# A matrix product with a written-out order: the last visit in two parts, two early stores whole, and a new order

## The chip, the cores and the metric

The kernel runs on one core of one Trainium2 chip. The metric is the device time of one execution in microseconds (us). An execution that was profiled has, beside this time, a span: the time from its first to its last instruction in the trace. All times below that are positions ("at 7.70") count from the start of the span.

## The reference

The inputs are `input` (16 × 512 × 1024) and `grad_output` (16 × 512 × 768), both float32. What is computed is

```python
grad_weight = np.einsum('bmk,bmn->kn', input, grad_output)
```

so with all 16 × 512 = 8192 rows in one list, the result is the product of the transposed input (1024 × 8192) with the gradient (8192 × 768): 1024 × 768 numbers, float32. The sum runs over the rows.

## The kernel before, in words

**Tiles.** The 8192 rows are cut in 64 slabs of 128, which is the depth of one matmul on TensorE. Two slabs are a pair; there are 32 pairs, u = 0 to 31 (line 12: pairs 0 to 3 are of the kind "s", the others of the kind "P"). The result is cut in 1024/128 = 8 row blocks and 2 halves of 384 columns. So one matmul takes 128 × 128 numbers of the input as the stationary operand (loaded into the array by a weight load, PEld) and 128 × 384 of the gradient as the moving one, and adds its product to 128 × 384 float32 numbers in one of the eight PSUM banks, bank 0 to bank 7.

**Fewer products.** The eight slabs of pairs 0 to 3 are multiplied in the plain way. The result's four quarters are named A, B, C and D (A and B are the upper 512 rows, A and C the left 384 columns), each with q = 0 to 3 for the row block inside. That is 16 matmuls for each slab. A pair of the kind "P" is treated as a 2 × 2 block product in Winograd's form: seven products in place of eight, named 1, A, B, C, 5, 6 and 7, each with q = 0 to 3, so 28 matmuls for each pair. Products 1 and A use the loaded tiles as they are. The others need sums of the tiles, which VectorE (DVE) makes: `sum_x` in three stages from x (lines 184, 186, 188) and `sum_g` in three from g (194, 196, 198). Products 5 and 7 need stage 0 of both, 6 needs stage 1, B needs stage 2 of x and C stage 2 of g. In all there are 8 × 16 + 28 × 28 = 912 matmuls of 384 columns.

**Loads.** Slab 0 and the x part of slab 1 come as float32 through the queues of SP and ACT, and DVE and ScalarE (ACT) round them to bf16 (line 202, tokens r0 to r4). Everything else is loaded by GpSimd's (POOL's) queue and becomes bf16 on the way (lines 153 to 160): for each pair first g, then x, in the order of u. Eleven pairs are held at a time, and eight sets of sums.

**Visits.** Eight kinds (A, B, C, D, 1, 5, 6, 7) with four q each make 32 sums, and there are eight banks. So a sum comes and goes: a *visit* opens a block in a bank, a number of matmuls are added to it, and the visit is closed, which copies the bank to SBUF (tile `acc` for A to D, `macc` for 1, 5, 6 and 7, `aside` for a part put by). When it comes again, either the stored sum is first copied back to the bank by ACT ("filled", line 309), or the visit starts at zero and DVE adds bank and stored sum when it is closed (line 378). A closing is done by ACT (a copy, line 356) or by DVE (line 376 a copy, 378 an addition). A0, A1 and A2 stay in banks 5, 6 and 7 for nearly the whole kernel.

**The end.** When a sum is complete, it is added to another (product 1 to A and 6, 6 to 7, 7 to C, 5 and others to B and D: DVE in lines 360 to 371, or POOL in line 388), and the part of the result is stored through SP's queue (line 291). The first `HALVED` stores are cut in two halves of 192 columns. The very last visits are B2 and B0; DVE's line 371 closes both.

**The order.** What each of PE, DVE, ACT and POOL does, and in which order, is written out by hand in the string `PLAN`: a list of tokens that is walked once, each engine taking its own instructions in this order. Each engine works strictly in order and waits at its next instruction until what it needs is there. The tokens:

- `C0@2.1`: visit of block C0 opens in bank 2 (from zero), with 1 matmul. `A0.3`: 3 more matmuls in A0's open visit. `@R` is the lasting bank of A0, A1, A2.
- `fB2@5`: ACT fills bank 5 with the stored B2. `fB2@0+3`: ACT fills columns 0 to 255 in bank 0 and columns 256 to 383 in bank 3.
- `cB2`, `vB2`, `kC2`: the visit is closed by ACT (c), by DVE (v), or by DVE with D's sum folded in (k).
- `x0.7`, `g2.7`: stage 0 of x, stage 2 of g for pair 7, on DVE.
- `pA3`, `qA3`: POOL adds the other sum, before the last visit is closed or after it.
- `r0` to `r4`: a rounding of slab 0 or 1.

`fill` knows visits in two parts: if two banks are named, the first takes 256 columns and the second 128. `multiply` then runs, for each part, all n matmuls of the token (so the weights are loaded once for each part), and `close` handles part by part; a final visit of B, C or D in two parts stores each part by itself, the left through SP's queue and the right through ACT's. The plan before has no such visit.

Ahead of everything, TensorE runs 17 matmuls on constants (`WARMUP`, line 136) while the first loads come.

Of the kernel before, what the change touches and what calls it, by code (L numbers as in the profile page):

```python
# [9 lines left out]
P = 128  # L10
# [4 lines left out]
    "C0@2.1 A0@R.1 r0 r1 r3 B1@1.1 r2 A2@R.1 r4 A1@R.1 vB1 A1.1 D3@4.2 A0.1 C0.1 D0@3.1 B2@0.1 cC0 B2.1 D0.1 "  # L15
    "fB1@1 A2.1 B3@2.2 cD3 B1.2 B3.1 D2@4.1 cB1 D2.1 vB3 D2.1 D0.1 A0.1 C1@2.3 C2@1.4 A1.2 cC2 B2.1 C1.1 B2.1 "
    "D2.1 cC1 D1@1.2 vD2 D1.1 fD3@2 D1.1 A2.2 cD0 vD1 B0@4.1 D3.2 A3@3.2 cD3 A3.2 B0.2 vA3 B0.1 C3@1.4 B2.2 "
    "B1@3.1 B0.1 cB2 B0.1 A1.2 cB0 D2@0.2 A0.3 D0@2.3 C3.2 A2.1 C0@4.1 vC3 C0.3 B1.2 B3@1.5 B1.1 D0.1 C0.1 vB1 "
    "C0.1 A0.2 vB3 D0.1 fD3@3 D2.2 vC0 fC3@1 A2.3 vD0 fD1@4 D3.3 vD2 D3.1 D1.1 g0.4 D1.1 fC1@0 D1.2 C3.1 fA3@2 "
    "g1.4 C3.1 C1.1 vD1 cD3 C1.3 kC3 fC2@3 A3.2 g2.4 A3.1 fB2@1 A3.1 x0.4 A3.1 C2.2 cA3 C2.1 x1.4 C2.2 A2.1 "  # L20
    "x2.4 10@2.1 cC2 A0.1 C1.1 v10 12@4.1 60@3.1 cC1 B2.1 g0.5 B2.1 c12 B2.1 61@0.1 g1.5 c60 62@2.1 B0@4.1 vB2 "
    "B0.1 c61 B0.1 11@3.1 c62 A1.1 vB0 A1.1 f12@1 A1.1 13@0.1 x0.5 13.1 12.1 11.1 c13 73@4.1 x1.5 73.1 c11 "
    "50@2.2 c12 k73 51@0.1 53@3.1 c50 53.1 x2.5 A1.1 52@4.1 g0.6 c53 52.1 51.1 fB1@2 A0.1 v52 63@1.2 c51 "
    "71@3.1 g1.6 71.1 fC0@4 g2.5 B1.2 g2.6 B1.1 c63 70@0.1 k71 70.1 C0.1 f10@1 C0.1 x0.6 C0.1 c70 B3@3.2 A1.1 "
    "cC0 10.1 x1.6 10.1 cB1 72@0.1 vB3 72.1 c10 72.1 C1@4.1 x2.6 f62@3 C1.1 60@2.1 k72 60.1 cC1 61@1.2 g0.7 "
    "A0.1 fB2@4 62.1 v61 62.1 B0@0.2 c62 g1.7 B2.2 vB0 c60 C3@1.2 cB2 C3.1 g2.7 C2@3.2 x0.7 fA3@2 C2.1 12@0.1 "
    "f51@4 12.1 vC3 A3.2 cC2 A3.1 v12 51.2 cA3 70@1.1 x1.7 70.1 c51 53@0.1 g0.8 53.1 A2.1 c70 A2.1 x2.7 A2.1 "
    "fB3@2 A1.1 v53 63@4.1 fB1@1 63.1 B3.1 g1.8 B3.1 f11@3 13@0.1 v63 13.1 cB3 B1.2 g2.8 11.1 v13 C3@4.1 cB1 "
    "C3.1 A2.1 x0.8 fC1@2s 11.2 C0@1.1 f71@0 C0.1 vC3 C1.2 cC0 71.1 x1.8 71.1 c11 71.1 vC1 52@1.2 c71 52.1 "
    "g0.9 A1.1 f73@3 60@4.2 v52 50@2.1 f62@0 50.1 g1.9 50.1 f13@1 73.1 v60 73.2 c50 62.1 x2.8 62.1 72@4.1 g2.9 "  # L30
    "72.1 c62 10@2.1 x0.9 10.1 c73 10.1 13.2 f70@0s v10 A0.2 f51@3 A0.1 v72 70.2 c13 51.1 x1.9 51.1 fC2@4s "
    "61@2.1 v70 61.1 fB2@1 61.1 C2.1 x2.9 C2.1 c51 B0@0.1 g0.10 B0.1 c61 B0.1 B2.1 vC2 B2.1 f11@3 B2.1 A2.1 "
    "vB0 f71@4 A3@2.2 x0.10 A3.1 cB2 11.1 A0.1 f12@0 11.1 g1.10 A2.1 71.1 f63@1 vA3 71.1 12.1 c11 12.1 g2.10 "
    "12.1 x1.10 c71 A1.2 g0.11 63.1 c12 63.2 fB1@4 x2.10 C1@3.2 g1.11 c63 62@2.2 vC1 B1.2 fB3@1 B1.1 v62 "
    "C0@0.1 fC3@3 C0.1 B3.1 g2.11 B3.1 cB1 B3.1 x0.11 C3.2 f72@4 C3.1 vC0 13@2.2 cC3 A2.1 x1.11 72.1 cB3 72.1 "
    "v13 72.1 f50@3s 73@0.2 g0.12 73.1 f53@1 52@2.2 v73 52.1 c72 50.2 g1.12 50.1 f60@0s 53.1 v52 53.1 fC0@4s "
    "53.2 g2.12 60.1 f51@2 v50 60.2 c53 A1.1 x0.12 A0.2 fB2@3 A1.1 C0.1 v60 f10@1 51.3 x1.12 C0.1 f70@0 10.2 "
    "vC0 c51 10.1 70.2 g0.13 70.1 f61@4s C2@2.2 x2.12 c70 C2.1 61.1 x2.11 c10 61.2 vC2 B2.2 f11@1 B2.1 g1.13 "
    "B0@0.1 f12@2 v61 B0.2 11.2 vB0 f62@4 11.1 12.2 cB2 x0.13 12.1 A3@0.1 c11 A3.2 g2.13 C1@3.1 f71@1 x1.13 "
    "C1.2 vA3 62.1 c12 62.2 g0.14 71.1 f63@0 71.2 x2.13 fC3@2 A2.1 63.1 vC1 63.1 c71 63.1 C3.1 g1.14 C3.1 c63 "  # L40
    "A2.1 g2.14 B3@1.1 c62 B3.2 x0.14 C3.1 A0.2 cC3 vB3 53@4.3 fB1@2 x1.14 73@0.2 v53 73.1 f72@1 50@3.2 x2.14 "
    "50.1 B1.1 v73 72.3 v50 60@4.2 c72 60.1 g0.15 B1.1 f52@0 B1.2 v60 13@3.3 A1.1 f70@4 x0.15 A1.2 cB1 52.2 "
    "v13 52.2 70.1 g1.15 70.1 c52 x1.15 70.1 A2.1 fC2@3 A2.1 g2.15 C0@0.1 g0.16 C0.1 c70 C0.1 C2.1 fB2@2 x2.15 "
    "C2.2 vC0 B0@4.2 cC2 B2.1 g1.16 B2.2 fC1@3 g2.16 51@1.2 vB0 51.1 cB2 12@0.2 x0.16 12.1 f10@4 C1.3 v51 10.2 "
    "cC1 10.1 x1.16 10.1 61@2.1 v12 61.1 c10 61.2 x2.16 f11@1 A1.1 71@0.1 g0.17 71.1 fB3@4 71.1 v61 62@3.3 v71 "
    "B3.3 v62 53@2.2 cB3 B1@0.1 g1.17 B1.1 11.1 v53 11.3 vB1 f60@2 A3@4.3 x0.17 c11 A3.1 A2.1 f72@3 A2.1 vA3 "
    "50@0.1 70@1.2 g0.18 72.1 f13@4 72.1 50.1 x1.17 50.1 72.1 v70 13.2 c72 13.1 g1.18 60.2 g2.17 c13 60.1 v50 "
    "63@1.1 fB2@3 63.2 g2.18 63.1 f73@0 A0.1 x0.18 A0.1 f52@4 A0.2 73.1 c60 x1.18 73.2 x2.17 73.1 52.1 x2.18 "
    "63.1 c73 C0@2.2 v63 C0.1 B0@0.2 vC0 B0.2 52.1 g0.19 52.1 fA3@2 A1.2 vB0 c52 B2.3 g1.19 f61@4 10@1.1 x0.19 "
    "10.2 A3.2 g2.19 51@0.2 x1.19 cA3 51.2 v10 cB2 A2.1 61.2 f62@2 v51 61.1 C1@3.2 x2.19 fC2@0 C1.1 62.1 g0.20 "  # L50
    "62.2 B1@1.1 vC1 B1.1 c62 C2.1 g1.20 B1.1 f53@3 A2.1 A1.1 g2.20 12@2.1 c61 vB1 12.3 f11@4 x0.20 C2.2 f70@1 "
    "C2.1 53.1 v12 53.1 cC2 53.2 x1.20 11.2 v53 A2.1 70.1 c11 70.1 x2.20 70.1 fB0@3 52@2.1 g0.21 52.1 B2@0.1 "
    "c70 B2.1 B3@4.1 g1.21 B3.1 v52 B3.2 B0.1 vB2 B0.1 C3@1.2 g2.21 C3.1 fC2@0 C3.1 vB3 C3.1 cB0 C3.2 A0.1 "
    "f72@2 A0.1 vC3 A0.1 13@4.1 C2.1 x0.21 13.1 f50@1 13.2 71@3.1 g0.22 71.2 x1.21 71.2 g1.22 72.3 g2.22 72.1 "
    "v71 50.2 c72 50.2 C2.1 x0.22 fC1@2 C2.1 13.1 A1.1 f60@3 A1.1 x1.22 A1.1 cC2 C1.2 v13 c50 C1.1 60.1 x2.21 "
    "60.1 cC1 60.1 x2.22 60.1 f63@0 60.1 C0@1.2 v60 C0.2 63.1 g0.23 63.3 vC0 A0.1 B0@3.1 c63 B0.1 g1.23 61@4.1 "
    "f51@1 61.2 x0.23 62@0.1 f11@2 62.1 51.1 vB0 51.3 x1.23 11.2 v61 11.2 61@3.1 A0.1 A2.1 v61 A2.2 62.1 v11 "
    "62.1 73@4.2 g0.24 f70@2 73.3 x2.23 c51 10@3.2 v62 10.1 fA3@1 10.2 x0.24 A1.2 70.2 x1.24 70.2 v10 50@0.3 "
    "x2.24 A3.2 v50 A3.3 v73 B1@3.1 fB3@0 B1.2 g2.23 cA3 B1.1 g0.25 B1.1 c70 B3.2 vB1 B3.1 f13@1 B3.1 12@2.1 "
    "g1.25 f53@4 12.2 x0.25 12.1 f52@3 12.1 53.2 vB3 53.2 x1.25 53.1 13.2 v12 13.1 52.1 g1.24 52.1 c13 52.1 "  # L60
    "g2.25 52.1 c53 52.1 x2.25 63@2.1 A0.1 f11@0 g0.26 63.2 B2@1.1 g1.26 11.2 v63 A2.2 B2.2 f60@2 x0.26 B2.2 "
    "c11 A0.1 B0@4.1 c52 B0.1 x1.26 B0.1 60.1 g2.24 fC2@0 60.1 g2.26 60.2 71@3.2 g0.27 c60 71.1 C2.2 x2.26 "
    "C2.2 vB0 C3@2.1 B2.1 A1.1 g1.27 fC0@4 A1.1 kC2 C3.3 g2.27 C3.1 f72@0 C0.2 x0.27 C0.3 vC3 71.3 kC0 72.1 "
    "fC1@2 72.2 vB2 72.1 fA3@4 72.2 x1.27 C1.2 c72 v71 C1.3 g0.28 f73@0 62@1.3 fB3@3 kC1 62.1 A0.1 73.1 g1.28 "
    "73.1 f51@2 v62 73.2 A3.1 g2.28 A3.2 x0.28 A3.1 52@1.2 cA3 51.1 x2.27 51.1 c73 51.1 x1.28 51.2 52.1 A1.1 "
    "50@0.1 v52 50.3 v51 61@4.1 f70@1 61.2 g0.29 61.2 70.1 g1.29 70.2 v61 70.1 A2.1 A1.1 v50 B3.1 f63@4 12@2.2 "
    "x0.29 12.1 63.3 x1.29 A2.2 g2.29 A2.1 70.1 x2.28 63.1 A0.1 v12 A0.2 B3.1 k70 B3.2 B1@0.1 x2.29 B1.1 cB3 "
    "B1.1 g0.30 B1.1 c63 B1.1 10@2.2 x0.30 f60@4 10.4 vB1 60.2 53@3.1 g1.30 53.2 x1.30 53.2 g2.30 13@0.2 v53 "
    "13.2 60.2 g0.31 f72@3 A1.2 f11@1 v10 A0.1 A2.1 72.1 g1.31 72.1 f12@2 72.1 11.1 g2.31 11.1 x2.30 11.2 "
    "x0.31 11.2 A1.1 13.1 c11 13.1 x1.31 12.1 cA1 12.1 v13 12.1 A0.1 f62@1 A2.1 x2.31 10@6.1 p63 c12 72.1 60.1 "  # L70
    "v10 cA2 62.3 cA0 62.1 v60 63@7.1 f73@6 63.1 qA0 v62 A3@0.1 f70@4 A3.1 73.1 v63 73.1 f50@5 73.2 qA2 v72 "
    "70.1 f53@2 A3.1 50.1 v73 70.1 fC3@3 53.1 50.1 v70 f61@1 qA1 50.1 C3.2 v53 fC2@7 C3.2 fB3@6 C3.1 pA3 61.2 "
    "cC3 61.1 v50 C2.1 f71@4 C2.3 qC3 f51@3 C2.1 v61 71.2 cC2 71.1 vA3 71.1 fC0@1 B3.1 qC2 B3.1 v71 B3.1 fB1@7 "
    "51.2 vB3 f52@0 51.1 C0.1 pC1 C0.1 fB0@4 v51 C0.2 fB2@5 C1@2.4 vC0 B1.2 52.1 vC1 52.2 vB1 B2.3 v52 B2.2 "
    "B0.4 vB2 B0.2 vB0 "
).split()

WARMUP = [("b", 512), ("f", 512), ("f", 512)] + 14 * [("b", 128)]
PAIRS_HELD = 11
SUMS_HELD = 8  # L80
MERGED = 2
HALVED = 4
ASIDES = 7
# [5 lines left out]
def kernel(  # L89
# [8 lines left out]
    f32 = mybir.dt.float32  # L98
# [4 lines left out]
    NH = N // 2  # L103
# [237 lines left out]
    def close(engine, p, q, queue):  # L341
# [39 lines left out]
        if last(p, q) and not opened[p, q] and not (engine == "c" and p in "ABC"):  # L381
            closed.add((p, q))
# [66 lines left out]
```

## Time and profile before

| | before |
|---|---|
| median of 3 runs | 161.49 us (161.28 to 161.57) |
| the profiled execution, its own time | 161.48 us |
| its span | 159.7 us |
| mean granted TensorE clock | 0.999 |
| matmuls of the product (L331) | 576 + 336 = 912, of 128 × 384 |
| busy: PE, DVE, ACT, POOL | 154.6, 136.1, 104.4, 42.6 us |
| loads by POOL's queue (q0) | 28.64 MB, 90.7% of 16 DMA engines' span |
| stores | 12 of 192 KB, 8 of 96 KB, all through SP |

How to read it. The lines of the profile name the line of the kernel (L331 is `nc.tensor.matmul` in `multiply`), the engine, the operation, what it writes and reads, how often, the busy time and the mean of one in ns. "Idle before" is how long the engine stood still just ahead of them, and whom it waited for. The view of waits sums that up by pairs of waiter and releaser: in total, how often, the longest. The chain of waits goes back from the last instruction to what released it, step by step. The timeline lists instructions in order of time, several of a kind in one line. A DMA has an issue, which is an instruction of a queue, and a landing, when its last byte is counted.

Two other things are used below. The *order* is what stands in the built program for each engine, one instruction after another; it has no times in it. From it every matmul has a number, 1 to 912. The *landings* are the times in the trace when each load was counted complete.

### The profile page before, as it was taken

How to read it: one execution, taken by the hardware profiler on the slowest of the kernel's cores; microseconds unless marked ns; L12 is line 12 of the kernel's file. 1: busy time of each engine (PE TensorE's matmuls, PEld its weight loads, DVE VectorE, ACT ScalarE, POOL GpSimd, SP SyncE). 2: the span in 40 equal slices, each digit the busy share in tenths (PEclk: the TensorE clock that was granted, in tenths of full speed). 3: DMA queues.
4: the chain of work that ended last, by engine and by line, in shares of the span. 5: the costliest groups of instructions: out<-in, count | busy, mean ns of one | idle time of the engine just before them, and what ended most of it. 6: DMA issues, size and time to landing. Idle time of an engine off the chain costs nothing.

```text
span 159.7 us, 2734 instructions
## 1 busy us (share of the span) xinstructions
PE 154.6 (97%) x931; PEld 91.2 (57%) x931; DVE 136.1 (85%) x316; ACT 104.4 (65%) x243; POOL 42.6 (27%) x77
## 2 busy tenths in 40 slices
PE   8899999999999999999999999999999999999990
PEld 3456656556555565665656565656566565656560
DVE  0514169999999999999999999989999899999992
ACT  3445238999999999967867585563465472339930
POOL 7442222222212222221222221222222100006930
PEclk9999999999999999999999999999999999999999
DMA  5999999999999999999999999999999999940696
GB/s 171 297 212 211 214 216 212 213 213 212 213 213 211 214 212 213 214 211 214 213 214 212 214 213 214 212 211 213 213 211 219 208 214 213 213 81 0 196 353 239
DMA packets 12829, 33.40 MB, mean 209 GB/s; under 512 B 1424, under 2 KB 4624, under 8 KB 12816
## 3 DMA queue, kind: packets, MB, share of 16 engines
q0 software_dynamic: 9360, 28.64, 90.7%
q1 hardware_dynamic: 3168, 3.54, 6.6%
q10 hardware_dynamic: 288, 1.05, 1.7%
q8 instruction: 7, 0.11, 0.3%
q14 instruction: 6, 0.05, 0.1%
HBM read 58.72 MB, written 3.15 MB: 387 GB/s over the span
## 4 chain that ended last, share of the span: by engine, by line
PE 91%; DMA 4%; DVE 2%; issue 1%; ACT 0%; ACTq 0%; DVEq 0%
PE bank L331 91%; DMA xf<-in_input_dram 4%; DVE acc L371 1%; DVE macc L364 0%; DVE xp L202 0%; ACT macc L356 0%; ACTq L129 0%; DVE acc L378 0%; DVE acc L366 0%; DVEq L371 0%
## 5 line engine op out<-in xcount | busy, mean ns | idle before, releaser
L331 PE MATMUL bank<-gp,xp 128*128 128x384 bf16 x576 | 105.4, 326 | 0.7 <-DVE xp L202 0.6
L331 PEld LDWEIGHTS <-xp 128*128 128x128 bf16 x576 | 55.8, 98 | 39.1 <-DVE xp L202 1.0
L331 PE MATMUL bank<-ge,xe 128*128 128x384 bf16 x336 | 65.9, 326 | 0.0
L331 PEld LDWEIGHTS <-xe 128*128 128x128 bf16 x336 | 32.7, 98 | 22.3 <-DVE xe L184 0.6
L309 ACT COPY bank<-macc 128x384 f32<-128x384 f32 x69 | 32.6, 489 | 10.4 <-DVE macc L378 6.2
L356 ACT COPY macc<-bank 128x384 f32<-128x384 f32 x64 | 29.4, 484 | 10.4 <-PE bank L331 10.1
L378 DVE TENSOR_TENSOR macc<-bank,macc 128x384 f32<-128x384 f32 x56 | 30.5, 554 | 1.2 <-PE bank L331 0.9
L154 POOL DMA_DIRECT2D xp<-in_input_dram x30 | 15.9, 529 | 52.6 <-DMA xp<-in_input_dram 21.9
L309 ACT COPY bank<-acc 128x384 f32<-128x384 f32 x46 | 21.8, 485 | 11.5 <-DVE acc L378 8.9
L356 ACT COPY acc<-bank 128x384 f32<-128x384 f32 x44 | 20.7, 480 | 11.4 <-PE bank L331 11.1
L153 POOL DMA_DIRECT2D gp<-in_grad_output_dram x30 | 15.9, 531 | 38.4 <-PE bank L331 17.2
L378 DVE TENSOR_TENSOR acc<-bank,acc 128x384 f32<-128x384 f32 x42 | 22.8, 553 | 1.9 <-PE bank L331 1.9
L184 DVE TENSOR_TENSOR xe<-xp 128x1024 bf16<-128x1024 bf16 x28 | 19.3, 689 | 1.0 <-DMA xp<-in_input_dram 0.9
L194 DVE TENSOR_TENSOR ge<-gp 128x768 bf16<-128x768 bf16 x28 | 15.5, 552 | 0.2 <-DMA gp<-in_grad_output_dram 0.2
L376 DVE COPY acc<-bank 128x384 f32<-128x384 f32 x9 | 5.0, 555 | 8.9 <-PE bank L331 8.9
L186 DVE TENSOR_TENSOR xe<-xe,xp 128x512 bf16<-128x512 bf16 x28 | 11.8, 421 | 0.3
L188 DVE TENSOR_TENSOR xp<-xp,xe 128x512 bf16<-128x512 bf16 x28 | 11.5, 419 | 0.0
L196 DVE TENSOR_TENSOR ge<-gp,ge 128x384 bf16<-128x384 bf16 x28 | 9.9, 353 | 0.2
L198 DVE TENSOR_TENSOR gp<-ge,gp 128x384 bf16<-128x384 bf16 x28 | 9.8, 354 | 0.2
L388 POOL TENSOR_TENSOR acc<-acc,macc 128x384 f32<-128x384 f32 x7 | 6.8, 1003 | 0.5 <-ACT acc L356 0.5
L388 POOL TENSOR_TENSOR macc<-macc 128x384 f32<-128x384 f32 x1 | 1.0, 1042 | 18.0 <-DVE macc L378 18.0
L202 DVE CAST gp<-gf 128x192 bf16<-128x192 f32 (+1 forms) x2 | 0.6, 310 | 4.9 <-DMA gf<-in_grad_output_dram 4.9
(23 smaller groups left out, 41.2 us busy)
## 6 DMA issues: line engine op xcount, KB each, us to landing
xp<-in_input_dram POOLq DMA_DIRECT2D x30, 512.0 KB, 16.7
gp<-in_grad_output_dram POOLq DMA_DIRECT2D x30, 384.0 KB, 16.7
out_dram<-acc SPq DMA_DIRECT2D x12, 192.0 KB, 2.1
xf<-in_input_dram ACTq DMA_DIRECT2D x2, 512.0 KB, 4.9
out_dram<-acc SPq DMA_DIRECT2D x8, 96.0 KB, 1.7
gp<-in_grad_output_dram POOLq DMA_DIRECT2D x3, 192.0 KB, 6.4
xp<-in_input_dram POOLq DMA_DIRECT2D x2, 256.0 KB, 7.8
gf<-in_grad_output_dram SPq DMA_DIRECT2D x2, 192.0 KB, 4.1
```

What stands on the lines that cost most here:

```text
L153: nc.gpsimd.dma_start(out=gp, in_=G[rows, :].rearrange("(p m) n -> p m n", m=2))
L154: nc.gpsimd.dma_start(out=xp, in_=X[rows, :].rearrange("(p m) k -> p m k", m=2))
L184: nc.vector.tensor_sub(out=xe[:, 0:2, :], in0=x[:, 1::-1, :], in1=x[:, 3::-2, :])
L186: nc.vector.tensor_sub(out=xe[:, 2, :], in0=xe[:, 0, :], in1=x[:, 0, :])
L188: nc.vector.tensor_add(out=x[:, 1, :], in0=x[:, 2, :], in1=xe[:, 2, :])
L194: nc.vector.tensor_add(out=ge[:, 0:2, :], in0=g[:, 0:2, :], in1=g[:, 1::2, :])
L196: nc.vector.tensor_add(out=ge[:, 2, :], in0=g[:, 3, :], in1=ge[:, 0, :])
L198: nc.vector.tensor_add(out=g[:, 1, :], in0=ge[:, 2, :], in1=g[:, 2, :])
L309: nc.scalar.copy(out=tile_[:, at : at + c1 - c0], in_=src[:, c0:c1])
L331: nc.tensor.matmul(tile_[:, at : at + c1 - c0], stat, mov[:, c0:c1], start=fresh, stop=True, skip_group_check=True,)
L356: nc.scalar.copy(out=to, in_=b)
L378: nc.vector.tensor_add(out=to, in0=b, in1=to)
```

## The change

The diff changes the string `PLAN` throughout, two numbers, the banks of the warm-up, and how a closing by ACT of a block that POOL has already added to is treated. (The new plan has no such closing: its `p` tokens are pA3 and p70, and both visits are closed by DVE.)

```diff
 PLAN = (
-    "C0@2.1 A0@R.1 r0 r1 r3 B1@1.1 r2 A2@R.1 r4 A1@R.1 vB1 A1.1 D3@4.2 A0.1 C0.1 D0@3.1 B2@0.1 cC0 B2.1 D0.1 "
...
-    "51.2 vB3 f52@0 51.1 C0.1 pC1 C0.1 fB0@4 v51 C0.2 fB2@5 C1@2.4 vC0 B1.2 52.1 vC1 52.2 vB1 B2.3 v52 B2.2 "
-    "B0.4 vB2 B0.2 vB0 "
+    "C0@0.1 A1@R.1 A0@R.1 r0 C1@3.1 B1@4.1 B3@1.1 r1 r4 cC1 B3.1 A2@R.1 r3 A2.1 vB3 C0@2.1 vC0 r2 D3@0.2 "
+    "C3@1.3 C0.1 A1.1 cC3 A1.1 vC0 C2@3.2 D3.1 A0.2 cD3 C2.1 C1@2.2 vC2 D1@0.4 fB3@3 A3@1.4 C1.1 B3.1 vA3 B3.1 "
...
+    "71.1 v61 71.1 fC1@6 71.2 v52 cB3 71.1 C2.1 f51@7 C2.1 qB3 C2.2 fB1@2 v71 C2.1 51.1 fB2@0+3 51.1 vC2 B1.3 "
+    "fB0@1 v51 C1.4 B0.2 vC1 B0.3 vB1 B2.3 vB0 B2.5 vB2 "
 ).split()
...
-HALVED = 4
+HALVED = 3
...
-    wps = psum.tile([P, 512], f32, name="bank7")
-    for dt, cols in WARMUP:
+    wps = [psum.tile([P, 512], f32, name=f"bank{b}") for b in (7, 4)]
+    for n, (dt, cols) in enumerate(WARMUP):
...
-            wps[:, 0:cols],
+            wps[n % 2][:, 0:cols],
...
+                assert (p, q) not in prepared or (final and carried and len(parts) == 1)
                 nc.scalar.copy(out=to, in_=b)
...
-        if last(p, q) and not opened[p, q] and not (engine == "c" and p in "ABC"):
+        if final and engine == "c" and (p, q) in prepared:
+            store(p, q, 0, NH, queue)
+        if last(p, q) and not opened[p, q] and (engine != "c" or p not in "ABC" or (p, q) in prepared):
             closed.add((p, q))
```

With `HALVED` 3 in place of 4, one store of 192 KB that was two issues of 96 KB is one. The last visit is now B2's, with eight matmuls for each of its two parts (`fB2@0+3`, `B2.3`, `B2.5`), 256 columns and 128 columns wide. So TensorE has 904 matmuls of 384 columns, 8 of 256 and 8 of 128. Ahead of it stand C1's last visit (4 matmuls), B0's (5, the first two before vC1) and, in DVE's order, v51, vC1, vB1 and vB0. SP has 6 stores of 192 columns, 12 of 384 and one of 256; ACT's queue has one of 128, the right part of B2. The order of POOL's loads is as it was; the last additions on POOL are eight as before (two p, six q, for three and five).

At the start, the first eleven matmuls are C0, A1, A0, C1, B1, B3 on slab 0, then B3 on slab 1, A2 on slab 0, A2 and C0 on slab 1, and D3 on slab 0 in bank 0. On DVE the first closings are vB3 (bank 1) and then vC0 (bank 0).

## The prediction

> **What bounds the kernel now.** I began with the page: its engine line and chain of waits say that TensorE is nearly all of the span.
>
> ```profile
> PE 154.6 (97%) x931; PEld 91.2 (57%) x931; DVE 136.1 (85%) x316; ACT 104.4 (65%) x243; POOL 42.6 (27%) x77
> PE 91%; DMA 4%; DVE 2%; issue 1%; ACT 0%; ACTq 0%; DVEq 0%
> q8 instruction: 7, 0.11, 0.3%
> ```
>
> A busy PE does not say that more work could have been done sooner, so I listed the starts of the 912 real matmuls (L331). The first starts at 5.91 us, the 912th at 155.75. A step between two that nothing delays is 0.1625 us (mean of 895 of the 911 steps), so 911 of them are 148.0 and 1.8 us are stalls: 1.0 before 7.70, the rest in a few steps, of which the view of waits names these:
>
> ```profile
> PEld L331 <- DVE xp L202: 1.0, 1, 1.0
> PEld L331 <- DMA xp<-in_input_dram: 1.0, 4, 0.3
> PEld L331 <- DVE xe L184: 0.6, 2, 0.4
> ```
>
> TensorE waits for loads and for the sums made from them, in the middle of the kernel. The loads come at a rhythm of their own: the x part of pair u lands at 16.16 (u=2), 20.50, 25.60, 29.91 and then every 4.31 us (47.44 for u=9, 64.70 for 13, 138.03 for 30, 142.53 for 31). One pair is 28 matmuls, 4.55 us of TensorE: little more than the rhythm of its load.
>
> So I made one table from the orders and the landings. If the first matmul that needs load u is number n, the 912th can't start before E = landing + 0.05 + (912 − n) × 0.1625; the 0.05 is the usual delay from landing to first use (51.75 to 51.79, 34.22 to 34.27). If it needs a sum made by L184, add 0.69 for that and 0.05 for its wait. For the kernel before, the largest E is 155.75, from pair 27: x lands at 125.70, 0.62 later than the rhythm asks, and matmul 732 needs its sum. 125.70 + 0.05 + 0.69 + 0.05 leaves 126.49, and 180 × 0.1625 = 29.25 more is 155.74. The 912th started at 155.754: this one landing set the end. The next largest E that the same late landing does not touch is 155.31 (u=10). The timeline shows the place, first DVE and then the weight loads:
>
> ```profile
> 125.73 0.69 DVE L184 TENSOR_TENSOR xe<-xp 128x1024 bf16<-128x1024 bf16 x1 [0.70 <-DMA xp<-in_input_dram]
> ```
> ```profile
> 126.47 0.93 PEld L331 LDWEIGHTS <-xe 128*128 128x128 bf16 x7 [0.38 <-DVE xe L184]
> ```
>
> DVE idles 0.70 for the landing, TensorE then 0.38 for DVE.
>
> Behind the last matmul stand an addition and a store, in the chain by order of time:
>
> ```profile
> 155.55 0.55 DVE acc L371
> 156.12 0.56 DVE acc L371
> ```
>
> The last addition begins 0.363 after the start of the last matmul and ends at 156.68, the store is issued at 156.70 and lands at 158.80; the closing waits end at 159.70. The profiled execution took 161.48, so 1.78 lies outside the span; 161.48 is also the median of the runs shown (161.49) to 0.01.
>
> **The change, part by part.**
>
> *The start.* What moves:
>
> ```profile
> 7.14 0.50 DVE L202 CAST xp<-xf 128x256 bf16<-128x256 f32 x2 [0.76 <-DMA xf<-in_input_dram]
> 7.14 0.71 ACT L202 CAST xp<-xf 128x256 bf16<-128x256 f32 x2 [1.73 <-DMA xf<-in_input_dram]
> 7.55 0.55 DVE L376 COPY acc<-bank 128x384 f32<-128x384 f32 x1
> ```
>
> Before, five matmuls run on slab 0, and the sixth waits for the second DVE cast until 7.70. After, six run (5.91 to 6.88, g's right half being cast by 6.38), and the seventh (B3) needs ACT's first cast only: 7.55 + 0.05 = 7.60. But vB3 stands ahead of vC0 in DVE's order: vB3 begins 0.363 after matmul 7, at 7.97; vC0 follows 0.47 later and ends at 8.99; and matmul 11 (D3) wants bank 0, which vC0 empties. It starts at 9.04 in place of 8.25, so 0.79 is lost. Onward at one step each (slab 2 is needed at 9.69 and lands at 9.63, slab 3 at 12.1 and lands at 11.88) number 36 starts at 13.05, where the kernel before has number 39. That gives E = 13.05 + 876 × 0.1625 = 155.40: half a microsecond later than before's own start (154.92), and under the largest E of the loads, so it costs nothing by itself.
>
> *The loads.* The same loads are issued by POOL in the same order, with buffers free over 16 us before they land, so I take the landings of before. First uses and E in the new order: u=2 n=55, 155.47; u=5 139, 155.57; u=6 166, 155.50; u=9 247, 155.55; u=13 353, 155.59; u=19 513, 155.46; u=22 593, 155.40; u=27 730, 155.33; u=30 805, 155.46; u=31 833, 155.41. The sums give no more: 155.47 (u=9, n=252), and for pair 27 only 154.76, since its first user is matmul 738. So the late landing that set the end is now covered, but the rest has moved up: the line is flat, 155.59 at most, 0.16 under 155.75.
>
> *Banks and engines.* DVE has five evictions fewer (124 tokens "v" for 129), ACT nine copies fewer (230 for 239). The shortest distances in the order, from the end of a bank's eviction or fill to the next matmul in it, are four matmuls in both kernels, apart from D3 above. Before, one such wait cost 0.25 (at 88.9, for ACT), beneath a cover of 0.5. The cover is now 0 to 0.2. A stall of this kind can cost from 0 to 0.25; I take 0.10, and 155.69 in place of 155.59.
>
> *Warm-up.* Its two banks in turn add no instruction; the 17 warm-up matmuls end when the first real one starts. If the turn cost time it would have the 0.19 between 155.40 and 155.59 as cover.
>
> *The last visit.* Call the start of its first matmul T0: 154.617 before; after, 155.69 − 7 × 0.1625 = 154.55. Eight matmuls of 384 columns become eight of 256 and eight of 128. A warm 128-column step is 0.058 (the last warm-ups, 5.738, 5.796, 5.854). For 256 no row exists: between 0.058 and 0.1625; I take the line through both, 0.110. Order: 3 of 256, 3 of 128, 5 of 256, 5 of 128. The last 256 starts at T0 + 0.94, the last 128 at T0 + 1.29 (before: 1.14). An addition starts 0.20 after its matmul has streamed, so the 256-column addition can start at 1.25, with vB0 gone by 0.89. Additions of 256 and 128 columns are not in the trace: between the casts of that size (0.30 and 0.28) and the 0.55 of 384; I take 0.42, and 0.29 by the row of the same size. They end at 1.67 and, the second following 0.08 before the first is done, 1.88 (before: 2.06).
>
> *The stores.* SP's queue is a part of this: 6 halves, 12 whole and one of 256 columns, each about 0.47 or 0.50 after the last. The first waits for POOL's addition of A1 (about slot 861 of the matmuls), and 6 × 0.473 + 12 × 0.497 = 8.8 us later SP is free, at T0 + 1.76: just behind the addition. One half fewer saves 0.45 there; without it the end would be that much later. A 256-column store is 128 KB:
>
> ```profile
> out_dram<-acc SPq DMA_DIRECT2D x12, 192.0 KB, 2.1
> out_dram<-acc SPq DMA_DIRECT2D x8, 96.0 KB, 1.7
> ```
>
> between these I take 1.85. It lands at T0 + 3.61; the 64 KB on ACT's queue, at 1.7 or less, by 1.90 + 1.65 = 3.55. (ACT's only DMA rows, 512 KB loads of 4.9, were slow in a crowd in which SP's 192 KB loads took 4.1, so 2.1 is its upper end.) Before: 158.80 = T0 + 4.18. Gain 0.57.
>
> The Trainium skill, page "DMA: Bandwidth & Descriptors", section "Anatomy of one DMA — SWDGE (gpsimd) path", speaks against the split: about 2.0 us of a DMA are fixed and only bytes / 436 GB/s scale. By it a third off the last store saves 0.15 and the sum would be 0.1 higher; the rows differ by 0.4 for 96 KB, where it gives 0.23, and I go by the rows.
>
> **Sum:** 0.06 by T0 and 0.57 by the tail: 161.48 − 0.63 = **160.85 us**.
>
> **Rivals.** 0.2% is 0.32 us, about what a measurement of this kernel can tell from no change: 161.17 and 161.81 are the bounds.
>
> 1. *A late landing on the flat line*, 161.4, chance 0.20. Pair 27's 0.62 comes right behind one of queue 8's 16 KB transfers (it starts at 123.67 and takes 0.96; the others start at 21.04, 42.42, 62.27, 83.27, 104.21 and 143.18). TensorE's order is longer by 16 instructions, all at the end, so the fetches should stay with the same pairs. If one moves onto a pair of the line, 155.59 + 0.62 = 156.21 gives 161.37. For it: ten rows of the line lie within 0.2. Against: 62, 83 and 104 left no late landing. The Trainium skill, "Runtime: NRT & Kernel Launch", section "Instruction fetch mechanics", calls these refills of 16 KiB, 256 instructions, mostly hidden. Size and spacing agree here; hidden the one at 123.67 was not, as far as its place shows.
>
> 2. *The store's time doesn't shrink with its size*, 161.10, chance 0.10: 2.1 for either part leaves T0 + 3.86, a gain of 0.32. The 1.7 of the halves speaks against it.
>
> 3. *Slower: the load stream falls back for good*, about 161.9, chance 0.11. Behind the fetch at 21.04, pair 4's g came 0.87 late and 0.79 stayed in every later landing; at 42.42 another 0.28 stayed. The new start runs 0.5 us later through just this place. One more such pair of steps lifts the whole line by 1.07: 160.85 + 1.07 = 161.92. It decides from 0.96 on; in the order before, whose line had 0.4 free, the same would cost 0.6.
>
> 4. The split isn't what it says: no chance worth a number, since the built order shows both parts, SP's store waiting for the first addition and ACT's for the second.
>
> Forecast 0.59. The range reaches from no stall, a line 0.2 lower and a tail 0.1 cheaper (160.4) to rival 1 with its additions and stores at their upper ends (161.7). Faster than 161.17: forecast and rival 2, 0.69; within the bounds: rival 1, 0.20; slower: rival 3, 0.11.
>
> **What would show it.** Matmul 11 at 9.0 and an idle PE before it; the first use of pair 13 within 0.1 of its landing; no wait at pair 27; the last 384-column matmul at about 154.4; the last two additions near 0.42 and 0.29; the last landing 3.6 behind T0. Wrong it is if landings stand elsewhere than at 4.31 us, if a bank wait of over 0.2 lies behind pair 13, or if SP is still working off older stores when the split's first addition ends.

## The result, and the profile after

| | before | after |
|---|---|---|
| median of 22 runs each, same chip | 161.33 us (161.12 to 161.57) | 162.76 us (161.44 to 163.27) |
| the profiled execution | 161.48 us, span 159.7 | 161.51 us, span 159.7 |

The ratio of the means is 1.0073, with a 95% interval of 1.0058 to 1.0087: slower, where 160.85 was forecast. And the changed kernel's times are two groups with nothing between them: 5 runs at 161.44 to 161.65 (the *lower group*) and 17 at 162.51 to 163.27 (the *upper group*). The kernel before, run in turns with it, has one. The profiled execution of the changed kernel belongs to the lower group, so it can't show what made the median; it does show how the steps of the forecast came out. The engines, the chain by engine and the instruction queue:

```profile
PE 153.8 (96%) x939; PEld 91.8 (57%) x939; DVE 135.9 (85%) x312; ACT 102.1 (64%) x235; POOL 42.6 (27%) x77
PE 92%; DMA 4%; DVE 1%; issue 1%; DVEq 0%; POOLq 0%
q8 instruction: 7, 0.11, 0.3%
```

TensorE is busy for 0.8 us less, and the span is the same. The chain by order of time, start to end (start, us, what):

```profile
1.24 6.39 DMA gp<-in_grad_output_dram
...
7.67 0.35 PE bank L330
...
8.04 1.03 DVE acc L376 x2
...
9.12 146.60 PE bank L330 x905
155.72 0.02 issue
155.75 0.42 DVE acc L371
```

The start is as forecast: the seventh matmul at 7.67 (7.60), vB3 and vC0 as one piece of 1.03, and D3 behind them at 9.12 (9.04). From there 905 matmuls follow in one piece, where the last unbroken piece of before's chain begins only at 88.94, behind an ACT copy. The stores on the page:

```profile
out_dram<-acc SPq DMA_DIRECT2D x12, 192.0 KB, 2.2
...
out_dram<-acc SPq DMA_DIRECT2D x6, 96.0 KB, 1.7
```

The last visit starts (T0) at 154.50, forecast 154.55. The steps of 256 and 128 columns take 0.109 and 0.056, DVE's two additions 0.42 and 0.28, and DVE is done at T0 + 1.87 (1.88). But the 128 KB store, issued at T0 + 1.76 as forecast, takes 2.32 to its landing, and the 64 KB one 2.37: the last landing is at T0 + 4.27, before at 4.18, where 3.61 was forecast. So the lower group lacks the 0.57 of the tail, and the upper group is another 1.2 us behind it.

### The profile page after: what moved, and what is told of

The parts are those of the page before. It is cut to its first block, busy times and chain, and to the rows that moved or that the text cites. A ratio compares the mean times of both kernels' runs of the same rounds, so it can differ in the third digit from the quotient of the medians.

```text
span 159.7 us, 2730 instructions
## 1 busy us (share of the span) xinstructions
PE 153.8 (96%) x939; PEld 91.8 (57%) x939; DVE 135.9 (85%) x312; ACT 102.1 (64%) x235; POOL 42.6 (27%) x77
## 4 chain that ended last, share of the span: by engine, by line
PE 92%; DMA 4%; DVE 1%; issue 1%; DVEq 0%; POOLq 0%
PE bank L330 92%; DMA gp<-in_grad_output_dram 4%; DVE acc L376 1%; DVE acc L371 0%; DVEq L446 0%; POOLq L435 0%
## 5 line engine op out<-in xcount | busy, mean ns | idle before, releaser
L330 PE MATMUL bank<-gp,xp 128*128 128x384 bf16 (+2 forms) x584 | 104.4, 324 | 1.4 <-DMA gp<-in_grad_output_dram 0.7
L330 PE MATMUL bank<-ge,xe 128*128 128x384 bf16 x336 | 64.7, 326 | 0.0
L330 PEld LDWEIGHTS <-xe 128*128 128x128 bf16 x336 | 32.9, 98 | 21.7
L356 ACT COPY macc<-bank 128x384 f32<-128x384 f32 x59 | 27.2, 481 | 12.0 <-PE bank L330 11.3
L356 ACT COPY acc<-bank 128x384 f32<-128x384 f32 x45 | 21.2, 483 | 19.9 <-PE bank L330 19.7
L308 ACT COPY bank<-macc 128x384 f32<-128x384 f32 x62 | 29.2, 487 | 5.3 <-DVE macc L378 2.6
L378 DVE TENSOR_TENSOR macc<-bank,macc 128x384 f32<-128x384 f32 x55 | 29.7, 551 | 0.9 <-PE bank L330 0.6
L308 ACT COPY bank<-acc 128x384 f32<-128x384 f32 (+2 forms) x49 | 23.3, 482 | 8.5 <-DVE macc L378 5.0
L152 POOL DMA_DIRECT2D gp<-in_grad_output_dram x30 | 16.0, 532 | 38.9 <-PE bank L330 20.7
L378 DVE TENSOR_TENSOR acc<-bank,acc 128x384 f32<-128x384 f32 x39 | 21.3, 551 | 5.7 <-PE bank L330 5.6
L376 DVE COPY acc<-bank 128x384 f32<-128x384 f32 x10 | 5.5, 554 | 3.4 <-PE bank L330 3.3
L371 DVE TENSOR_TENSOR macc<-bank,macc 128x384 f32<-128x384 f32 x7 | 3.7, 548 | 0.0
```

The lines of the kernel that those rows point to most:

```text
L152: nc.gpsimd.dma_start(out=gp, in_=G[rows, :].rearrange("(p m) n -> p m n", m=2))
L308: nc.scalar.copy(out=tile_[:, at : at + c1 - c0], in_=src[:, c0:c1])
L330: nc.tensor.matmul(tile_[:, at : at + c1 - c0], stat, mov[:, c0:c1], start=fresh, stop=True, skip_group_check=True,)
L356: nc.scalar.copy(out=to, in_=b)
L378: nc.vector.tensor_add(out=to, in0=b, in1=to)
```

## The experiments

All are comparisons of five rounds beside the kernel before, whose median was 161.33 to 161.42 in every one. Letters in the expectations: A is the theory that queue 8's first transfer (the refill of TensorE's instructions) takes the place of pair 3's load when it comes too early, and that the number of instructions ahead decides it; B lays the upper group to the tail (e1 to e3), later to the new order or the loads themselves (e5 to e7); C lays it to the clock. S lays the end to SP's issuing, T to the rate of the DMA engines; R and F are explained where they stand.

### Where the upper group comes from

**e1_same**: the changed kernel once more, no edit.

> The changed kernel once more, for the times of more executions and for a profile of one that takes near 162.8 us (the 22 times on record lie in two groups, 5 near 161.5 and 17 near 162.8, and the profiled one is of the first group). Theory A, the load stream falls back for good early on: in an execution near 162.8 every landing from about pair 4 or 5 on stands 1.0 to 1.3 us later than in the profile of before, the first use of each pair follows at 0.05, and the tail is the same. Theory B, the tail: landings as before, the last matmul near 155.8, and the stores or the two last additions 1.2 us later. Theory C, the clock: a stretch after the idle time at 6.8 to 9.1 us in which a 384-column matmul takes 0.32 in place of 0.16, landings as before.

Measured: 162.74, ratio 1.0062 (1.0039 to 1.0086); five runs at 161.38 to 161.67, seven at 162.72 to 163.03. The groups are the kernel's own. Its profile (161.67) again showed the lower one.

**e2_whole_last**: the last visit whole.

```diff
-fB2@0+3
+fB2@0
```

> The changed kernel with its last visit whole (fB2@0 in place of fB2@0+3): 8 matmuls of 384 columns, one addition, one store through SP. Theory A and C: two groups of times as in the changed kernel, near 161.5 and 162.8, median within 0.3 us of it. Theory B: only the first group, 161.4 to 161.8. For the tail by itself: if SP's stores, one behind the other, set the end, the whole visit is at most 0.2 slower than the split one; if the split is worth the 0.57 of the prediction, 0.4 to 0.6 slower within each group.

Measured: 162.72, ratio 1.0091 (1.0078 to 1.0104); all five runs in the upper group, the profiled one too. So at last a trace of it. TensorE's weight loads from 20 to 23 us (start, us, what, and in brackets the idle time before and whom for), first of the changed kernel's lower group, then of this run:

```profile
19.94 0.58 PEld L330 LDWEIGHTS <-xp 128*128 128x128 bf16 x4
20.70 2.26 PEld L330 LDWEIGHTS <-xp 128*128 128x128 bf16 x15 [0.17 <-DMA xp<-in_input_dram]
```
```profile
19.95 0.59 PEld L330 LDWEIGHTS <-xp 128*128 128x128 bf16 x4
22.02 0.93 PEld L330 LDWEIGHTS <-xp 128*128 128x128 bf16 x7 [1.49 <-DMA xp<-in_input_dram]
```

Both are about to start matmul 82, the first that uses pair 3. Its x lands at 20.66 in the one and at 21.98 in the other; the loads behind it land at their usual times. The prediction's own line then says what this costs: 21.98 + 0.05 + 830 × 0.1625 = 156.91, and the 912th matmul of e2 starts at 156.914. The chain of waits of e2 goes through this landing and nothing behind it:

```profile
7.92 14.07 DMA xp<-in_input_dram
21.98 0.05 issue
22.03 135.22 PE bank L330 x831
```

One landing, 1.3 late, is the whole upper group. The profiles of e3 and e7 below, in the upper group too, show the same: x of pair 3 at 21.91 and 21.88. (Of the changed kernel without an edit no profile fell in the upper group.) That leaves nothing for the clock (C), since the 830 steps behind it take 0.1625 each, nor for the tail (B): the last landing is at T0 + 4.19. What stands beside the late landing is queue 8's transfer. The DMA view of e2 from 19.6 to 20.6, which has both queues (packets, MB, share of 16 engines):

```profile
q0 software_dynamic: 74, 0.19, 97.7%
q8 instruction: 1, 0.02, 5.9%
```

It starts at 19.95 there and at 20.01 and 20.06 in the two lower-group profiles; in the kernel before at 21.04, behind the landing.

**e5_fewer**: 16 instructions of TensorE fewer in the warm-up, ahead of everything.

```diff
-WARMUP = [("b", 512), ("f", 512), ("f", 512)] + 14 * [("b", 128)]
+WARMUP = [("b", 512), ("f", 512), ("f", 512)] + 2 * [("b", 512)] + 4 * [("b", 128)]
```

> The changed kernel with 16 instructions fewer ahead of its order on TensorE: of the warm-up's 14 matmuls of 128 columns 10 are left out and 2 of 512 columns put in, about the same time. Profiles near 162.8 show x of pair 3 landing at 21.9 to 22.0 in place of 20.5 to 20.7, matmul 82 waiting 1.3 us for it, and all else as in those near 161.6; queue 8's first 16 KB transfer starts at 19.9 there and, in the kernel before, at 21.0. Theory A, this transfer makes x3 late, and its place goes with the count of TensorE's instructions: 16 fewer move it 8 matmuls (1.3 us) back, behind x3: all executions 161.3 to 161.8, none near 162.8, x3 at 20.5 to 20.7. Theory B, the new order of the first 82 matmuls or the loads themselves make x3 late: about three in four near 162.8, as before the edit.

Measured: 161.61 (161.49 to 161.95, 11 runs), ratio 1.0016 (1.0007 to 1.0025). The upper group is gone (B would have kept it). The transfer starts at 22.71, x of pair 3 lands at 20.49.

**e6_old_more**: the kernel before with 20 instructions more, so that its transfer comes early.

```diff
-WARMUP = [("b", 512), ("f", 512), ("f", 512)] + 14 * [("b", 128)]
+WARMUP = [("b", 512), ("f", 512), ("f", 512)] + 24 * [("b", 128)]
```

> The kernel before with 10 more warm-up matmuls of 128 columns (20 instructions, 0.6 us, hidden in its idle time up to 7.7 us). Theory A: queue 8's first transfer comes 10 matmuls (1.6 us) sooner, at about 19.4 to 20.0, and makes x3 land near 21.9 in many executions; matmul 86 waits, and 21.95 + 0.05 + 826 x 0.1625 = 156.2 in place of 155.75 for the last matmul: a second group near 161.8 to 161.9. Theory B: 161.1 to 161.6 as before, x3 at 20.5.

Measured: 162.31 (162.09 to 162.50), ratio 1.0059 (1.0046 to 1.0071): the old order made ill in the same way. The transfer starts at 19.70, x of pair 3 lands at 21.78, and TensorE waits for it:

```profile
21.82 1.25 PEld L331 LDWEIGHTS <-xp 128*128 128x128 bf16 x9 [1.29 <-DMA xp<-in_input_dram]
```

The time is 0.4 over what was expected. By the landing alone the 912th matmul would start at 21.78 + 0.05 + 826 × 0.1625 = 156.06; it starts at 156.53, because the old order's own waits come on top, 0.05 at matmul 144, 0.15 at 206 and 0.25 at 502, as in before's profile. That an early transfer goes with a late x of pair 3 holds on both orders, cured in one and brought about in the other.

**e7_more**: the changed kernel with `28 * [("b", 128)]`, 28 instructions more.

> The changed kernel with 14 more warm-up matmuls of 128 columns (28 instructions, 0.8 us in TensorE's idle time up to 7.6 us). Theory A: the first transfer comes 2.3 us sooner, about 17.7, and hits g of pair 3 (lands at 18.16, needed only with x3 at 20.7) in place of x3: all executions 161.3 to 161.8. Theory B: most near 162.8. If x3 is late still, the transfer's effect lasts longer than the 1.4 us behind it that pair 27 and others showed.

Measured: 162.69 (162.65 to 162.74), ratio 1.0082 (1.0070 to 1.0095), every run in the upper group. But the transfer starts at 19.80, 0.2 earlier than in the changed kernel and not the 2.3 that were expected.

**e17_eight_fewer** and **e18_four_fewer**: the changed kernel with 8 and with 4 instructions fewer.

```diff
+WARMUP = [("b", 512), ("f", 512), ("f", 512)] + [("b", 512)] + 9 * [("b", 128)]
```
```diff
+WARMUP = [("b", 512), ("f", 512), ("f", 512)] + 12 * [("b", 128)]
```

> The changed kernel with 8 instructions of TensorE fewer ahead of the loads of pair 3 (one warm-up matmul of 512 columns in place of five of 128, with their weight loads). Theory A (queue 8's first transfer makes the upper group when it starts ahead of the landing of x of pair 3): with 16 fewer it started at 22.7, with none fewer at 19.9 to 20.1. About 8 instructions later at 0.08 each is 20.6 or later, behind the landing at 20.5: one group, 161.5 to 161.7. If the place of the transfer jumps instead of shifting, it is at 20.0 as before and the two groups stay, most times at 162.5 to 163.

> The changed kernel with two warm-up matmuls of 128 columns fewer, which is 4 instructions of TensorE. Theory A with a shift of 0.08 per instruction: the transfer starts at 20.2 to 20.4, in time by what the executions so far show (late at 19.95 and before, in time at 20.01 and later), so most or all times are at 161.4 to 161.7. If it jumps: as the changed kernel, about three in four at 162.5 to 163.

Measured: 161.65 (161.54 to 161.90), ratio 1.0016 (1.0007 to 1.0025), and 161.56 (161.42 to 162.01), ratio 1.0018 (1.0008 to 1.0028); none of the 22 runs is in the upper group. The same stretch of e18's DMA view holds loads alone:

```profile
q0 software_dynamic: 80, 0.21, 106.0%
```

The transfer starts at 21.78 and 21.70. So two warm-up matmuls fewer move it by 1.7 us, in a jump, and cure the kernel. The shift in proportion, from the changed kernel's place on, that I had expected is refuted. The count is not without effect, though. In weight loads and matmuls of TensorE that had begun when the transfer started, warm-up included, it stands behind 209 to 221 of them in fifteen of the 20 profiles (e6 and e7, with 217 and 221, among them), behind 199 in e9, and behind 191 to 193 in the four with the new order and its full warm-up (the result's, e1, e2 and e3). So these four are early, and e18 is back in the common place. Why they are early stays open, and so does how a transfer of 0.9 us makes a load 1.3 late: the profiles show the two together, and that both move with the warm-up. Over all profiles the transfer starts at 19.70 to 20.06 or at 20.9 and later, never between, while x of pair 3 lands at 20.5 to 21.1 where it isn't late. Some times of e5, e17 and e18 lie at 161.7 to 162.0, a little over the lower group; of those no profile was taken.

### The start

**e3_vc0_first**: vC0 ahead of vB3, so that D3 doesn't wait.

```diff
-"... B3@1.1 r1 r4 cC1 B3.1 A2@R.1 r3 A2.1 vB3 C0@2.1 vC0 r2 D3@0.2 "
+"... B3@1.1 r1 r4 vC0 cC1 B3.1 A2@R.1 r3 A2.1 vB3 C0@2.1 r2 D3@0.2 "
```

> The changed kernel with vC0 ahead of vB3 on DVE (token vC0 moved behind r4), so that matmul 11 (D3 in bank 0) finds its bank free: TensorE loses no 0.8 us at 8.3 and stands 0.7 us earlier until the loads stop it at pair 2. Theory A with TensorE's early progress as its cause (the first 16 KB transfer of the instruction queue comes with TensorE's place in its order): the share of executions near 162.8 changes clearly, by more than half. Theory A with another cause (the order later on): shares as in the changed kernel. Theory C: only the group near 161.5 is left. Theory B: as the changed kernel.

Measured: 162.85, two runs at 161.47 and 161.56, six at 162.73 to 163.13; ratio 1.0079 (1.0053 to 1.0106). TensorE's first microseconds:

```profile
7.58 1.47 PE L330 MATMUL bank<-gp,xp 128*128 128x384 bf16 x8 [0.44 <-DMA gp<-in_grad_output_dram]
9.83 1.47 PE L330 MATMUL bank<-gp,xp 128*128 128x384 bf16 x8 [0.77 <-DMA xp<-in_input_dram]
```

The wait of 0.79 for vC0 is gone, and 0.77 of waiting for slab 2 has come in its place. The stall costs nothing, as forecast, and both groups are there without it.

### The tail

**e8_two_queues**: e5_fewer with the stores behind v51 and vB1 on ACT's queue (`v51a`, `vB1a`), to take load off SP.

> e5_fewer's warm-up, and of the last five whole stores two (D1 and B1) issued by ACT's queue in place of SP's. The tail of the changed kernel: SP issues 20 stores one behind the other, 0.5 us each, from 7.0 us ahead of the last visit on; the last one of 128 KB takes 2.3 to its landing, not 1.85. Theory S, SP's issuing holds the end: the last landing comes 0.4 to 0.8 us sooner after the start of the last visit than 4.27, and the time is 0.4 to 0.8 under e5_fewer's in the same group. Theory T, the 16 DMA engines work off the stores at their own rate (a whole store in 0.53): the last landing at 4.1 to 4.3, time within 0.15 of e5_fewer's.

Measured: 161.62 (161.40 to 161.78), ratio 1.0015 (1.0006 to 1.0024); e5 without it 161.61. The last landing is at T0 + 4.30 (4.27 in e5): S is refuted, and a queue more doesn't make the stores land sooner here.

**e11_no_a_split**: e5_fewer without A's four stores (that part of the output isn't written). **e12_no_a_whole**: the same with `fB2@0`.

```diff
+        if p == "A":
+            return
```

> e5_fewer without the stores of the quarter A (the first three, A3, A1, A2, and A0): its part of the output is not written, 12 stores in place of 16. Theory T, the stores stand in a row at 0.53 us each from the first on: without the four the row is worked off when the last parts come, the 128 KB and 64 KB of the split land 1.6 to 1.9 behind their issue, the last landing at 3.5 to 3.7 behind the start of the last visit in place of 4.27, time 0.5 to 0.75 under e5_fewer. If the parts land 2.3 behind their issue all the same, their own cost was mis-sized and no row: time within 0.15 of e5_fewer.

> e11_no_a_split with the last visit whole: again without the stores of A. Theory T: the addition of 384 columns ends at 2.06, the store of 192 KB lands 2.0 to 2.1 behind its issue, at 4.1 to 4.2, so 0.45 to 0.6 slower than e11_no_a_split: the split is worth what was predicted once no row of stores stands ahead of it. If the split is worth nothing by itself: within 0.15 of e11_no_a_split.

Measured: 161.58 (161.42 to 161.72), ratio 1.0012 (1.0004 to 1.0021), and 161.55 (161.42 to 161.87), ratio 1.0014 (1.0005 to 1.0022). The test failed in its design: SP still issued a store each half microsecond up to the last, so the row was shortened and not emptied, and the split was worth nothing as before. In the profiles the last landing does come sooner, at T0 + 4.03 split and 3.98 whole (4.27 in e5, 4.17 in e15 below), but what follows it to the end of the span takes 1.21 in place of 0.97.

**e13_lone_split** and **e14_lone_whole**: e5_fewer with B2's store alone (nothing else of the output is written), split and whole; `HALVED = 0` keeps this one store from being halved. R is the theory that the row of stores ahead sets the landing, F that a store has a fixed time whatever its size.

```diff
+        if (p, q) != ("B", 2):
+            return
```

> Leaves out every store but that of B2, so the other outputs are not written: the row of stores ahead of the last one is empty. The last visit is split as in the change, after the short warm-up that keeps the load of pair 3 in time. Theory R (a store's landing is set by the row of stores ahead of it on the DMA engines): now both parts land by the rows of single stores, the 128 KB one 1.85 after its issue, the 64 KB one 1.65 or less, so the last landing is at T0 + 3.6. Theory F (a store has a fixed time whatever its size): about 2.1 for either part, so T0 + 3.9 to 4.0. Rival: the time is a little under 161.6 only because the end is shorter.

> The same with the last visit whole: one store of 192 KB, none ahead of it. Theory R: it lands 2.0 to 2.1 after its issue, at T0 + 4.1 to 4.2, so the split gains about 0.5 over this kernel. Theory F: the same place, T0 + 4.15, and the split gains 0.15 to 0.25, from the earlier end of the addition alone. If the split gains nothing even here, the end is not set by the stores' landings at all.

Measured: 161.09 (160.76 to 161.19), ratio 0.9982 (0.9973 to 0.9990), and 161.24 (160.92 to 161.55), ratio 0.9993 (0.9984 to 1.0002). The DMA views from 155 to 159, forty slices of 0.1 us, the busy share of the engines in tenths: before, after, the lone whole store, the lone split one.

```profile
DMA  9899999899999998999999999998999993000000
```
```profile
DMA  8989899989999989999998998979998993000000
```
```profile
DMA  0000000000000000000000000299998200000000
```
```profile
DMA  0000000000000000000000028999992000000000
```

Before and after, the engines are full without a gap until 158.3: the last store's bytes stand behind those of the stores ahead of it. In how many parts, by which queue and 0.2 earlier or later they are issued moves the last landing by little: T0 + 4.17 whole (e15), 4.27 split (e5), 4.30 over two queues (e8). Alone, they find idle engines. Then issue to landing is, for the whole store (first) and for the parts:

```profile
out_dram<-acc SPq DMA_DIRECT2D x1, 192.0 KB, 1.9
```
```profile
out_dram<-acc SPq DMA_DIRECT2D x1, 128.0 KB, 1.7
out_dram<-acc ACTq DMA_DIRECT2D x1, 64.0 KB, 1.8
```

and in the changed kernel, in the row, from 155 on:

```profile
out_dram<-acc SPq DMA_DIRECT2D x3, 192.0 KB, 2.4
out_dram<-acc SPq DMA_DIRECT2D x1, 128.0 KB, 2.3
out_dram<-acc ACTq DMA_DIRECT2D x1, 64.0 KB, 2.4
```

Without the row the last landing is at T0 + 3.69 split and 3.96 whole: the split gains 0.27 there (0.15 between the medians), of which 0.19 is the earlier end of DVE's work and the rest the smaller size. With the row the two are at 4.27 and 4.17. So it costs the split parts 0.6 and the whole store 0.2, and that takes the split's gain away. That the row ahead counts is R; what the split gains without it is nearer to F's 0.15 to 0.25 than to R's 0.5. The forecast's 0.57 isn't there in either case.

**e15_whole**: e5_fewer with `fB2@0`, all stores kept.

> The changed kernel with the short warm-up and the last visit whole, all stores kept. Against the short warm-up alone (161.61): if the split is worth nothing behind a row of stores, as the comparison with the upper group of the changed kernel said, 161.5 to 161.65; if it was worth the forecast 0.57, 162.1 to 162.2.

Measured: 161.64 (161.36 to 161.90), ratio 1.0019 (1.0010 to 1.0028), against 161.61 with the split. The split is worth nothing in this kernel; in the profiles its last landing is 0.10 later behind T0.

**e10_halved4**: e5_fewer with `HALVED = 4`. (The change makes one early store whole, from 4 to 3, and not two as the title has it; this run takes it back.)

> e5_fewer with four halved stores as before, in place of three: one issue more in SP's queue. The prediction's term, SP's issues set the end: 0.4 to 0.5 slower than e5_fewer, last landing at 4.7 behind the start of the last visit. Theory T, the DMA engines' rate sets it and SP's issues are hidden: within 0.15 of e5_fewer, last landing at 4.2 to 4.35.

Measured: 162.60 (162.22 to 162.63), ratio 1.0072 (1.0058 to 1.0086), 1.0 over e5. SP issues the 128 KB store 0.47 later (T0 + 2.22), as the prediction said of one half more. But it lands only 0.38 later than e5's last landing; 0.23 more is T0 (154.72, where pair 18's x came late behind a transfer), and 0.37 the closing, since SP, which ends with eight waits one after another, has seven of them left at the last landing in place of one. These make 0.98, the difference between the two profiles; whether e10's other runs have the 0.23 as well, no profile shows. T alone is refuted: here the issues do reach the end.

### What the old order had

**e4_old_plan**: the kernel before with the warm-up in two banks and `HALVED = 3`. **e16_halved3**: with `HALVED = 3` alone.

> The plan of before with the small parts of the change alone: the warm-up on banks 7 and 4 in turn, three stores halved in place of four. All theories that lay the loss on the new order or on the split: 161.1 to 161.6, as before, in every execution. If a second group near 162.4 to 162.8 turns up here, the warm-up is its cause. The fourth store whole saves one issue of 0.45 us in SP's queue: if the stores' row sets the end, up to 0.3 faster than before.

> The kernel before with three stores halved in place of four, nothing else. With the warm-up in two banks as well it was 161.59, 0.25 over the kernel before. If the stores' number made that: 161.55 to 161.65. If the warm-up's two banks made it: 161.3 to 161.4.

Measured: 161.59 (161.33 to 161.84), ratio 1.0016 (1.0008 to 1.0025), and 161.46 (161.27 to 161.62), ratio 1.0004 (0.9994 to 1.0013). One group each, so neither part makes the upper group. Together they cost about 0.25; how much of it belongs to which part, e16 leaves open, since it lies between the two expectations.

**e9_old_fewer**: the kernel before with e5's warm-up.

> The kernel before with the shorter warm-up of e5_fewer (16 instructions fewer on TensorE). In e5_fewer every transfer of the instruction queue came 1.3 to 2.7 us later and x of pair 3 was in time. The line of the prediction: the kernel before is held by pair 27 alone, whose x comes 0.62 late behind the transfer at 123.67; moved to about 125, it leaves x27 at 125.1, and the next largest E is 155.31 in place of 155.75. So the 912th matmul starts at 155.3 to 155.5 and the time falls by 0.3 to 0.45: 160.9 to 161.1. Rival, the line is not what holds the end of the kernel before: 161.2 to 161.6, as before. If another pair near the line is hit instead, its lateness shows in its row and the time is as before or higher.

Measured: 161.40 (161.23 to 161.49), ratio 1.0001 (0.9992 to 1.0010). Pair 27 is in time, its x landing 4.31 behind the one before (4.94 in before's profile), and its wait is gone; that gained only 0.1 at the last matmul and nothing in the median. The chain goes back to an older wait:

```profile
88.47 0.49 ACT macc L356
88.96 0.04 issue
89.00 64.70 PE bank L331 x397
```

Before's chain has the same wait as its last one (its PE piece from 88.94 on) and nothing of pair 27, so it already named the next bound. Matmul 502 waits for ACT, and 89.00 + 410 × 0.1625 = 155.63 is the start of the 912th (155.636). Taken from before's own profile this bound is 88.945 + 66.63 = 155.57, so pair 27 stood 0.18 over the next bound there. And e16's profile, with the old plan, has pair 27 in time too, though the transfer starts at 123.67 as in before's: 161.27, with 88.75 + 66.63 = 155.38 for a last matmul at 155.39.

## Why the prediction was wrong

**The step that failed**, by the 1.2 us that make the median, is rival 1's "TensorE's order is longer by 16 instructions, all at the end, so the fetches should stay with the same pairs", and with it the size of the rival. The first transfer did not stay: it started at 21.04 before and at 19.88 to 20.06 in the new order. I had taken the danger to be pair 13's line, or a lasting shift of the stream behind the fetch (rival 3). It was pair 3, at the first transfer, and the lateness was not 0.62 but 1.3, for one load and not for the rest. The pair had little room: matmul 82 came up at 20.5 to 20.7, its load at 20.5 to 20.7 too. Pair 3 has no row among the ten that the prediction lists: 20.50 + 0.05 + 830 × 0.1625 = 155.43, so its load could be 0.26 late before it moved the forecast 155.69. In the old order, where matmul 86 is the first to use it, the same table gives 154.78, 0.97 under 155.75. The table itself would have shown the room that this load lost. Rival 1 in kind, at twice its price, is what happened in 30 of the 42 runs of e1, e3 and the result together, which gives it more than the 0.20 that I allowed; and at this price it ends beyond the range.

The Trainium skill, "Runtime: NRT & Kernel Launch", section "Instruction fetch mechanics", has the size of the refills right (16 KB each here), and its "mostly hidden" agrees with the result's profile, where no matmul behind the 15th starts more than 0.02 late. In the upper group the first one goes with a loss of 1.2 us, and TensorE waits there not for instructions but for a load that it needs at once.

**The second failure** is the tail: the term 0.57 was mis-sized; it measured 0 (e15 beside e5: 161.64 and 161.61). The times of the stores were read from medians over the whole row, and the halves' 1.7 was put down to their size. But the halves are the first of the row, when the engines have little ahead of them. What the 1.85 and 1.65 should have been read from is the DMA view of the end, which was there to be looked at: full until 158.3. In the last 3 us of before's profile a store of 192 KB lands 0.51 to 0.55 behind the one ahead of it. Rival 2 named a fixed time of the store, and would have given 0.32; on idle engines it came near, with 0.27, though 128 KB took 0.14 less than 192 KB there. Behind the row it doesn't hold either: the gain is 0.

The Trainium skill, "DMA: Bandwidth & Descriptors", section "Anatomy of one DMA — SWDGE (gpsimd) path", by which only bytes / 436 GB/s scale, gives an estimate of 0.15 for the 64 KB that the left part lacks. Its fit is for DMAs that GpSimd issues; these stores are SP's and ACT's. Still, the lone stores differ by 0.14 (1.87 and 1.73), where I went by the rows and took 0.25. The section says nothing of a row of stores ahead.

**What held.** T0 (154.50 for 154.55), D3's stall and that it costs nothing (e3), pair 27 covered, the steps of 256 and 128 columns, both additions, SP free at T0 + 1.76, and one half more for about 0.4 at the end (e10). The table of landings and remaining matmuls was right to 0.01 even for the upper group's profiles (e2, e3, e7); it was fed with the wrong landing. The start came out nearer to the line than forecast: matmul 36 stood at 13.27 in place of 13.05, which by the table is 155.62, level with pair 13's 155.63 in that profile.

**A third point, on the old kernel.** The stall that the table found at pair 27 was in the profiled execution, 161.48, which lies high among the 22 runs (median 161.33). The old plan's other profiles have no such stall. The list of the largest E held loads and sums and left the order's own waits out, so its next largest, 155.31 (u=10), should have been 155.57. The prediction had seen that wait, 0.25 at 88.9 for ACT, and put it "beneath a cover of 0.5"; the cover was 0.18. In e6 such waits add 0.45 to the bound of the late landing. The cover that I gave the old order, 0.4, was mostly not there, and its removal could not bring much. With the upper group cured (e5), the changed kernel is 0.2 over the old one; the last landing is 0.09 later behind T0 and the closing 0.06, and the rest lies within what one profile each can't tell apart.

No version that I ran and that computes the whole result beats the kernel before.

## What to carry to other kernels

Number the matmuls against the landings, and put the order's own waits into the same table: its largest row is the bound, and the next one says what its removal can gain. Before a new order is trusted, look which loads have no room at their first use, and run it several times, because a refill of instructions can come ahead of such a load or behind it; here four instructions fewer ahead of it decided that. And before the last store is cut or moved, look whether the DMA engines are idle when it is issued: while they were full here, neither the split (e15) nor a second queue (e8) brought the last landing forward, and leaving out stores ahead of it did (e11, e13).

## What I had not expected of the hardware

- Where one 16 KB transfer, 0.9 us long, starts at 19.70 to 19.95 (e6, e7, e3, e2), a load of 512 KB that is under way lands 1.3 us late; at 20.01 and 20.06 it doesn't, and at 20.9 and later pair 3's load is not touched. Four weight loads and matmuls of TensorE fewer, out of 1878, moved the start from 20.0 to 21.7 (e18). What sets the start is open.
- A store takes 1.7 to 1.9 us from issue to landing on idle engines, whether 64, 128 or 192 KB (e13, e14), and 2.1 to 2.4 at the end of a row (before, the result, e5, e15).
- SP's last waits cost 0.06 us each; how many are left at the last landing depends on the order of the stores (e10: 0.37).
